# Where the projections of the neighbourhood attention are emitted: behind the first recurrent mixer, or behind the gated recurrence

## The chip, the cores and the metric

The kernel runs on one core of a Trainium2 chip. The metric is the device time of one execution in microseconds (us); the median of three runs of the kernel before is 2086.45 us (2084.6 to 2095.07). TensorE (PE) multiplies matrices, VectorE (DVE), ScalarE (ACT) and GpSimd (POOL) do elementwise work, and DMA queues, issued here mostly by SyncE (SP) and ScalarE, move data between HBM and the on-chip memory.

## The reference

Two blocks run one after the other on 512 tokens of width 1024. The first (a dilated window attention and a gated delta rule) isn't touched here. The second block has three mixers side by side on one normalised input, then an output projection and a mixture of 32 experts. Cut to what matters:

```python
hl = rms_norm(xl, norm1_gain) * (1 + sc1l) + sh1l          # 512 tokens
hc = rms_norm(xc, norm1_gain) * (1 + sc1c) + sh1c          # 256 context tokens
pl, pc = hl @ w_in, hc @ w_in
al, bl, cl = split(pl, [A_PROJ, A_PROJ + B_PROJ])          # hgrn | rwkv | neighbourhood attention
a_lat = hgrn2_mixer(ac, al, ...)        # gated recurrence: chunk_gla in both directions, 4 heads
b_lat = rwkv7_mixer(bc, bl, ...)        # recurrence s = s*w - (s kk) ak + v k, both directions, 4 heads
c_lat = neighbourhood_attention(cc, cl, ...)   # 8 heads: softmax(q k + bias) v over an 8 x 16 window and the context
xl = xl + g1l * (concat([a_lat, b_lat, c_lat]) @ w_out)
xl = xl + g2l * hierarchical_moe(rms_norm(xl, norm2_gain) * (1 + sc2l) + sh2l, ...)
```

## The kernel before

It is one program written with a tile framework: Python emits the operations of each stage, a scheduler with priorities in the order of emission merges them into one fixed order per engine, and rotating buffers of named pools carry the dependencies. Once that order is fixed, every engine runs its own list strictly in order, so work "fills" an idle engine only where it stands in that engine's list between the instructions that wait.

The stages of the second block, in the order of emission:

- `rwkv_in` and `rwkv` (the first recurrent mixer, lines 960 to 1255): the 768 tokens are six blocks. For a block `j`, `front(j)` builds `KR`, `AH` and the matrix `AS` (L1068, L1118, L1120); four stores put `AS` into a scratch buffer (L1125, `rsc<-AS`), one load brings it back spread over all partitions (L1127, `rB<-rsc`); `solve32_rows` inverts it on VectorE in 31 steps of two instructions (L626, L627); four stores and four loads carry the result back into `AS` (L1145 `rsc<-sX`, L1148 `AS<-rsc`). `back(j)` starts with matmuls on that `AS` (L1157) and goes through `merge32` (L648, L652) and the state (L1166 to L1214). `front` runs one block ahead of `back`. A last part normalises and stores rows of `mix` (L1241 to L1255).
- `project` (L1277): the other projections. They are products of 128 output columns with `hl` (512 tokens) and `hc` (256 tokens), each made of three matmuls on split numbers (`mm3`, lines 314 to 316; the weights are split by ScalarE at L299 and GpSimd at L300). In this order: for the neighbourhood attention `w_na` (queries and keys, with sums of squares `nss` by a matmul at L1329) and `w_nv` (values); for the gated recurrence `w_hi` and `w_hg`. All results go to HBM. Being independent of `rwkv`, they are merged among its instructions.
- `hgrn` (the gated recurrence, L1368): loads `hfd`, `hkd`, `hqd`, `hvd`, `hgd`, then two pairs of heads with seven levels each, and a read-out into `mix` (L1545, L1552). Beside its levels runs `out_first`: the part of the output projection whose rows of `mix` are ready (weights `wor`, L1720; `g<-mrh,woh`).
- `na` (the neighbourhood attention): `prepare(p)` for four pairs of heads (tables `ntab`, loads `nt`, `nvt`, `nvw`, `nb`; lines 1562 to 1612), then four units a pair of scores (`ns`, L1637, L1639), softmax (`np`, L1643 on), transpose (`nT`, L1655) and values (`no`, L1670). `prepare(0)` is called from inside `hgrn` at its tenth step (`na_beside`).
- the rest of the output projection (`out_projection`), the router, and the experts, whose 201 MB of weights (`er`) stream in from 1542 us on.

The PSUM pool `gp` holds three buffers for the tag `g`, handed out in the order of emission: a projection can't begin before the buffer three tiles back is read out.

Of the kernel before, what the change touches and what calls it, by code (L numbers as in the profile page):

```python
# [10 lines left out]
F32 = mybir.dt.float32  # L11
F32R = mybir.dt.float32r
I32 = mybir.dt.int32
AF = mybir.ActivationFunctionType
# [125 lines left out]
def consts2():  # L140
    c = Pack()
    i = np.arange(P)
    c.add("ident", np.eye(P))
    bones = (i[:, None] // 64 == i[None, :] // 64).astype(np.float32)
    c.add("bones64", bones / 64)

    s, t = (i % 64)[:, None], np.arange(64)[None, :]
    c.add("rw_mask", np.concatenate([s < t, s <= t], 1).astype(np.float32))
    m = np.ones(T)
    m[63::64] = 0  # L150
    c.add("rw_reset", np.broadcast_to(m, (P, T)))
    sel = np.zeros((P, 4, 32))
    for h in range(8):
        sel[64 * (h % 2):64 * (h % 2) + 64, h // 2, h] = 1 / 64
    c.add("na_sel", sel)
    return c


def consts3():
    c = Pack()  # L160
    i = np.arange(P)
    c.add("ident", np.eye(P))
    c.add("bones64", (i[:, None] // 64 == i[None, :] // 64) / 64)
# [7 lines left out]
    f = np.arange(TC) % P  # L171
    c.add("hg_suf", np.broadcast_to((f != P - 1).astype(np.float32), (P, TC)))
    c.add("hg_pre", np.broadcast_to((f != 0).astype(np.float32), (P, TC)))
    return c
# [65 lines left out]
def prep2(i):  # L240
# [4 lines left out]
    o["c2"], o["c3"] = C2.array(), C3.array()  # L245
# [27 lines left out]
class Kern:  # L273
# [698 lines left out]
    def rwkv_in(self):  # L972
# [4 lines left out]
        nc.vector.tensor_scalar(m2, mu, 0.5, None, OP.mult)  # L977
        self.rw_wl = rw.tile([P, 768], F32, name="wlo")
# [41 lines left out]
    def rwkv(self):  # L1020
# [35 lines left out]
        def front(j):  # L1056
# [19 lines left out]
            nc.vector.tensor_tensor_scan(es[:, ::-1], sg[:, 1:T + 1][:, ::-1], self.c("rw_reset")[:, ::-1], 0.0, OP.add, OP.mult)  # L1076
# [34 lines left out]
            mask = self.c("rw_mask")  # L1111
# [165 lines left out]
    def project(self):  # L1277
# [4 lines left out]
        self.hqd, self.hgd = dram("hqd", 2, P, T), dram("hgd", 2, P, T)  # L1282
        self.hfd, self.hkd, self.hvd = dram("hfd", 2, 2, P, N), dram("hkd", 2, 2, P, N), dram("hvd", N, 256)
        self.nqk, self.nkc, self.nvd = dram("nqk", 4, 2, P, T), dram("nkc", 4, P, TC), dram("nvd", TC, T)
        self.nvw = dram("nvw", 4, 4, 64, 2, P)
        self.nqr, self.nkr = dram("nqr", 8, T), dram("nkr", 8, N)
# [33 lines left out]


# [18 lines left out]
        tokens(I["w_hi"], lambda i, o: rows(self.hvd, i, o))  # L1340


        l = self.v("lb")
        lb, nb = (self.gs.tile([P, 4], F32, name=n) for n in ("hlb", "hnb"))
        nc.vector.tensor_sub(lb, l, l)
        nc.scalar.activation(lb, lb, AF.Exp)
        nc.vector.reciprocal(nb, lb)
        nc.vector.tensor_mul(lb, lb, nb)
        nc.vector.tensor_sub(lb, lb, lb)
        nc.vector.tensor_scalar(nb, lb, -1.0, 1.0, OP.mult, OP.add)  # L1350
        for p in range(2):
            columns(I["w_hg"][p], self.hqd[p])
        for p in range(2):
            for d in range(2):
                c = 2 * d + p
                ps = self.gemm2(I["w_hg"][2 + c])
                f, k = st(N), st(N)
                for o, sign in ((f, 1.0), (k, -1.0)):
                    for x, t in zip((o[:, :TC], o[:, TC:]), ps):
                        nc.scalar.activation(x, t, AF.Sigmoid, scale=sign)  # L1360
                nc.vector.tensor_scalar(f, f, nb[:, c:c + 1], lb[:, c:c + 1], OP.mult, OP.add)
                nc.vector.tensor_scalar(k, k, nb[:, c:c + 1], None, OP.mult)
                nc.sync.dma_start(self.hfd[p, d], f)
                nc.sync.dma_start(self.hkd[p, d], k)
        for p in range(2):
            columns(I["w_hg"][8 + p], self.hgd[p], func=AF.Silu)

    def hgrn(self):  # L1368
# [167 lines left out]
        self.heads = self.na()  # L1536
        for i, p in enumerate(self.h_order):
            next(steps[p], None)
            for _ in range(self.na_beside.count(i)):
                next(self.heads)  # L1540
# [170 lines left out]
    def out_first(self):  # L1711
# [519 lines left out]
    def run(self):  # L2231
# [5 lines left out]
        self.na_beside = [9]  # L2237
# [9 lines left out]
        with ExitStack() as es:  # L2247
# [19 lines left out]
            with ExitStack() as e2:  # L2267
                for n in ("p2", "gs"):
                    pool(e2, n)
                pool(e2, "gp", 3, space=PSUM)  # L2270
                with ExitStack() as e3:
                    pool(e3, "tw")
                    self.block2_in()
                right.close()
                right = es.enter_context(ExitStack())
                pool(right, "rw", side="right")
                for n, b in (("rmp", 2), ("rcp", 2)):
                    pool(right, n, b, space=PSUM, side="right")
                self.rwkv_in()
                self.wq = nc.scalar  # L2280
                self.rwkv()
                self.project()
            ew.close()
            pool(es, "pc3")
            self.cst, self.cat = self.pc3.tile([P, C3.n], F32, name="c3"), C3.at
            nc.gpsimd.dma_start(self.cst, self.I["c3"])
            self.wq = nc.sync
            left = es.enter_context(ExitStack())
            pool(left, "nw")
            right.close()  # L2290
            pool(left, "nmp", space=PSUM)
            with ExitStack() as e2:
                e3 = e2.enter_context(ExitStack())
                pool(e3, "tl", side="right")
                with ExitStack() as e4:
                    pool(e4, "o1", side="right")
                    self.x = self.tl.tile([P, KD, T], F32, name="x1b")
                    self.out_at = (1, 1), (1, 1), (1, 3), (1, 3), (1, 5), (1, 5), (1, 6)
                    with ExitStack() as e5:
                        pool(e5, "hw", side="right")  # L2300
                        pool(e5, "hmp", 4, space=PSUM, side="right")
                        self.hgrn()
                e4 = e3.enter_context(ExitStack())
# [10 lines left out]
                left.close()  # L2314
# [31 lines left out]
```

## Time and profile before

| | |
|---|---|
| median of three runs | 2086.45 us |
| the profiled execution | 2096.92 us, span 2094.9 us |
| PE busy | 1841.7 us (88% of the span) |
| DVE, ACT, POOL busy | 970.0, 676.9, 579.8 us |
| chain that ended last | PE 32%, DMA 16%, issue 11%, DVE 7% |

The profile gives one execution of the program. A page of it has busy time by engine, the span in slices, and the chain of work that ended last, followed back from the last instruction. All times of the rows below are microseconds from the start of the span. "PEclk" is the granted clock of TensorE as a share of 2.4 GHz; "DMA share" is the mean busy share of the 16 DMA engines. Matmuls overlap in their pipeline, so the pace of a row of them is read from their starts, not from their durations. The profiled execution is 10.5 us longer than the median of the runs.

### The profile page before, as it was taken

To read this page: it belongs to the slowest core of one execution; us is meant where nothing else is said; L and a number is where in the kernel's file an instruction comes from. 1 tells how busy PE (TensorE), PEld (TensorE's weight loads), DVE (VectorE), ACT (ScalarE), POOL (GpSimd) and SP (SyncE) were. 2 spreads that over 40 slices of the span, in tenths; PEclk is the share of its full clock that TensorE was granted. 3 is DMA by queue.
4 is the path that set the end of the run, shared out by engine and by line. 5 is a ranking of instruction groups with operands and counts; after the bars stand their busy time and mean duration, and the time that the engine had idled before them with its cause. 6 is when DMAs were issued, how large, how long until landed. Compare 5 with 4: busy or idle time off the path is not lost.

```text
span 2094.9 us, 30479 instructions
## 1 busy us (share of the span) xinstructions
PE 1841.7 (88%) x11941; PEld 1304.6 (62%) x11941; DVE 970.0 (46%) x2047; ACT 676.9 (32%) x1246; POOL 579.8 (28%) x407
## 2 busy tenths in 40 slices
PE   5988899889899999889998999558896999999986
PEld 4665576666657777767687877436675554545442
DVE  5433643676673116435666544577666322222110
ACT  6662325543443234442232214534332111000000
POOL 3222412343446554341111111562101100101011
PEclk9877799899989999998778779669997999999999
DMA  3111223455642335222212123723356899999997
GB/s 131 41 50 36 76 61 112 131 177 192 199 141 78 94 109 191 64 81 70 66 37 68 44 64 96 245 94 116 100 221 260 324 412 415 414 416 412 415 413 278
DMA packets 132862, 363.69 MB, mean 174 GB/s; under 512 B 44110, under 2 KB 63726, under 8 KB 108014
## 3 DMA queue, kind: packets, MB, share of 16 engines
q1 hardware_dynamic: 122206, 340.86, 44.2%
q10 hardware_dynamic: 5472, 15.05, 2.6%
q0 software_dynamic: 5040, 5.82, 1.4%
q8 instruction: 95, 1.56, 0.3%
q14 instruction: 49, 0.40, 0.1%
HBM read 333.02 MB, written 26.55 MB: 172 GB/s over the span
## 4 chain that ended last, share of the span: by engine, by line
PE 32%; DMA 16%; issue 11%; DVE 7%; ACT 4%; POOL 4%; SPq 0%; POOLq 0%; ACTq 0%; DVEq 0%
DMA out_dram<-ey,sidx 13%; PE g L316 6%; PE g L314 6%; PE g L315 6%; DVE sX L627 1%; PE rm L1118 1%; POOL lo L300 1%; DVE stmp L626 1%; PE rm L1068 1%; PE gu L2144 1%; ACT hi L299 1%; DMA wor<-in_w_o_dram 1%; PE tr L2080 1%; DMA nt<-nqk 1%; PE no L1670 1%
## 5 line engine op out<-in xcount | busy, mean ns | idle before, releaser
L300 POOL TENSOR_TENSOR lo<-wraw,hi 128x1024 fp32r<-128x1024 f32 (+1 forms) x127 | 299.1, 2356 | 587.1 <-ACT hi L299 516.7
L314 PE MATMUL g<-h1hi,hi 128*128 128x512 f32 (+1 forms) x584 | 253.7, 434 | 11.7 <-ACT gt L441 7.5
L316 PE MATMUL g<-h1hi,lo 128*128 128x512 f32 (+1 forms) x584 | 250.7, 429 | 6.6 <-POOL lo L300 6.6
L315 PE MATMUL g<-h1lo,hi 128*128 128x512 f32 (+1 forms) x584 | 253.0, 433 | 3.1 <-DVE h1lo L357 1.6
L2144 PE MATMUL gu<-er,xw 128*64 128x256 f32 x2048 | 237.6, 382 | 11.3 <-DMA er<-in_w_e_dram 10.0
L299 ACT ACTIVATE hi<-wraw 128x1024 fp32r<-128x1024 f32 (+1 forms) x127 | 127.4, 1004 | 315.1 <-PE g L315 172.6
L2144 PEld LDWEIGHTS gu<-er,xw 128*64 128x64 f32 x2048 | 145.3, 137 | 98.8 <-issue 17.8
L2173 POOL DMA_INDIRECT out_dram<-ey,sidx x32 | 49.9, 1561 | 454.0 <-DVE ey L2172 454.0
L314 PEld LDWEIGHTS g<-h1hi,hi 128*128 128x128 f32 (+1 forms) x584 | 118.6, 203 | 46.9 <-ACT gt L441 8.4
L316 PEld LDWEIGHTS g<-h1hi,lo 128*128 128x128 f32 (+1 forms) x584 | 117.8, 202 | 44.4 <-POOL lo L300 11.4
L315 PEld LDWEIGHTS g<-h1lo,hi 128*128 128x128 f32 (+1 forms) x584 | 118.1, 202 | 38.4 <-issue 8.7
L2169 PE MATMUL py<-er,es 128*64 128x512 f32 x512 | 121.3, 606 | 1.5 <-SPq L2215 1.0
L314 PE MATMUL g<-hlhi,hi 128*128 128x512 f32 x200 | 85.2, 426 | 4.7 <-ACT hlhi L951 4.6
L2147 ACT ACTIVATE eg<-gu 128x256 f32<-128x256 f32 x32 | 12.2, 384 | 238.8 <-PE gu L2144 238.8
L2080 PE MATMUL tr<-h,S 128*128 128x512 f32 x256 | 75.0, 423 | 12.3 <-DVE xw L2089 7.1
L316 PE MATMUL g<-hlhi,lo 128*128 128x512 f32 x200 | 85.2, 426 | 0.0
L315 PE MATMUL g<-hllo,hi 128*128 128x512 f32 x200 | 85.2, 426 | 0.0
L2172 DVE SCALAR_TENSOR_TENSOR ey<-py,wslot,g2row 128x512 f32<-128x512 f32 x32 | 24.0, 751 | 120.5 <-PE py L2169 120.5
L2169 PEld LDWEIGHTS py<-er,es 128*64 128x64 f32 x512 | 34.3, 137 | 61.4 <-issue 53.3
L2148 DVE TENSOR_TENSOR eh<-eg,gu 128x256 f32<-128x256 f32 x32 | 13.3, 417 | 127.0 <-ACT eg L2147 127.0
L2080 PEld LDWEIGHTS tr<-h,S 128*128 128x128 f32 x256 | 46.1, 196 | 39.6 <-issue 20.5
L898 DVE CUSTOM_DVE_ANT_0 aw<-aw,acc 128x1024 f32<-128x1024 f32 x48 | 64.7, 1354 | 8.1 <-DMA aw<-in_w_ada_dram 7.8
(658 smaller groups left out, 3700.5 us busy)
## 6 DMA issues: line engine op xcount, KB each, us to landing
er<-in_w_e_dram SPq DMA_DIRECT2D x192, 1024.0 KB
aw<-in_w_ada_dram SPq DMA_DIRECT2D x48, 512.0 KB
wraw<-in_w_qkv_dram SPq DMA_DIRECT2D x36, 512.0 KB
wraw<-in_w_g_dram SPq DMA_DIRECT2D x12, 512.0 KB
dxs<-draw SPq DMA_DIRECT2D x96, 64.0 KB
wraw<-in_w_rw_dram SPq DMA_DIRECT2D x9, 512.0 KB
wraw<-in_w_ga_dram SPq DMA_DIRECT2D x8, 512.0 KB
wraw<-in_w_gb_dram SPq DMA_DIRECT2D x8, 512.0 KB
```

The costliest lines, as they stand in the source:

```text
L299: nc.scalar.activation(hi, raw, AF.Copy)
L300: (lo_engine or nc.gpsimd).tensor_sub(lo, raw, hi.bitcast(F32))
L314: nc.tensor.matmul(ps, lh, rh, start=start, stop=False, **kw)
L315: nc.tensor.matmul(ps, lh, rl, start=False, stop=False, **kw)
L316: nc.tensor.matmul(ps, ll, rh, start=False, stop=stop, **kw)
L626: nc.vector.tensor_mul(t, X[:, 0:m, u:u + 1].to_broadcast([P, m, w]), B[:, u:u + 1, u + 1:].to_broadcast([P, m, w]))
L898: nc.vector.tensor_tensor_reduce(out=w, in0=w, in1=cc, scale=1.0, scalar=0.0, op0=OP.mult, op1=OP.add, accum_out=self.modl[:, m:m + 1])
L2080: nc.tensor.matmul(ps[:n], S[:, i, :n], self.h2[i][a][:, c], start=i + a == 0, stop=i + a == 4)
L2144: nc.tensor.matmul(ps[64 * c:64 * c + 64, a, :], xs(2 * i + k), w[:, k, a, c, :], start=i + k + a == 0, stop=i == 3 and k == 1 and a == 1, ...
L2169: nc.tensor.matmul(py[64 * c:64 * c + 64], hs[:, k, 64 * i:64 * i + 64], part[:, k, c, :], start=i + k == 0, stop=i + k == 2)
L2172: nc.vector.scalar_tensor_tensor(y, py, w, self.g2, OP.mult, OP.mult)
L2173: nc.gpsimd.indirect_dma_start(out=self.O["out_0"].rearrange("t (h d) -> (t h) d", h=2), out_offset=bass.IndirectOffsetOnAxis(ap=idx, axis ...
```

## The change

`project` gets an argument. `project(True)` stands where `project()` stood and emits only `w_hi` and `w_hg`. `project(False)` emits `w_na`, the sums and `w_nv` after `hgrn()`. The constants `c3`, the pools of `na` and its first step (`prepare(0)`), which were emitted ahead of `hgrn` or inside it, come after that. `out_first` takes its PSUM tiles from `gp` (three buffers, shared with the projections) in place of two of `nmp`, since `nmp` is opened later. The constants `rw_mask` and `rw_reset` get an array of their own, loaded in `rwkv_in`; two constants of `hgrn` move to the array that is loaded first.

```diff
+def consts_rw():
+    s, t = (np.arange(P) % 64)[:, None], np.arange(64)[None, :]
+    m = np.ones(T)
+    m[63::64] = 0
+    return np.concatenate([s < t, s <= t, np.broadcast_to(m, (P, T))], 1).astype(np.float32)
...
+        self.rw_c = rw.tile([P, P + T], F32, name="rwc")
+        nc.sync.dma_start(self.rw_c, I["c_rw"])
...
-            mask = self.c("rw_mask")
+            mask = self.rw_c[:, :P]
...
-    def project(self):
+    def project(self, first):
...
+        if first:
...
+            tokens(I["w_hi"], lambda i, o: rows(self.hvd, i, o))
...
+            for p in range(2):
+                columns(I["w_hg"][8 + p], self.hgd[p], func=AF.Silu)
+            return
...
         for hf in range(2):
             tokens(I["w_nv"][2 * hf:2 * hf + 2], lambda i, o: window_rows(hf, i, o))
-        tokens(I["w_hi"], lambda i, o: rows(self.hvd, i, o))
...
-        self.heads = self.na()
-        for i, p in enumerate(self.h_order):
+        for p in self.h_order:
             next(steps[p], None)
-            for _ in range(self.na_beside.count(i)):
-                next(self.heads)
...
-            ps = [self.nmp.tile([P, T], F32, tag="ns", name=self.name("g"), bufs=2) for _ in range(2)]
+            ps = [self.gp.tile([P, T], F32, tag="g", name=self.name("g")) for _ in range(2)]
...
-                self.project()
-            ew.close()
-            pool(es, "pc3")
...
+            self.rwkv()
+            self.project(True)
+            right.close()
...
                         self.hgrn()
+                        self.project(False)
+                        ew.close()
+                        self.wq = nc.sync
+                        pool(left, "pc3")
...
+                        pool(nl, "nmp", space=PSUM)
+                        self.heads = self.na()
+                        next(self.heads)
```

What this moves in the engines' lists is not seen in the diff. Three places matter.

The first is TensorE's list where `back` of the fourth block (counted from one) begins in `rwkv`; `g` are projection tiles, `hlhi` and `hllo` the split input, `rm`, `pw`, `px` belong to the recurrence. Before:

```order
L1157 MATMUL rm_8277<-c_5995,AS_7690 32x32 x16
L314 MATMUL g_9866<-hi_9870,hlhi 128x256
L315 MATMUL g_9866<-lo_9871,hlhi 128x256
L316 MATMUL g_9866<-hi_9870,hllo 128x256
...
L648 MATMUL pw_8296<-rXT_8276,AS_7690 32x32 x8
```

The same place now (`_8279` is the same tile under its new number):

```order
L584 MATMUL rm_8152<-c_5995,rt_8150 64x64
L586 MATMUL rm_8152<-c_5995,rt_8150 64x64
L1161 MATMUL rm_8279<-c_5995,AS_7692 32x32 x16
L650 MATMUL pw_8298<-rXT_8278,AS_7692 32x32 x8
L654 MATMUL px_8300<-AS_7692,rt_8299 32x32 x8
```

The projections that remain have run out: from `back` of the third block to the end of `rwkv` no projection matmul is left in the list.

The second is the end of `hgrn` on TensorE, where `hm` are its last matmuls. Before, the scores `ns` of the neighbourhood attention stand between them:

```order
L1524 MATMUL hm_11171<-hPT_10625,hvt 64x128 x2
L1637 MATMUL ns_11352<-nk_10945,nq_10935 128x256
L1637 MATMUL ns_11353<-nk_10945,nq_10935 128x256
L1499 MATMUL hm_11206<-c_10448,hE_10538 128x128 x4
L1499 MATMUL hm_11213<-c_10448,hE_10539 128x128 x3
L1527 MATMUL hm_11172<-hlf_10478,hS_11136 64x128
```

Now:

```order
L1530 MATMUL hm_10343<-hPT_9839,hvt 64x128 x3
L1530 MATMUL hm_10343<-hPT_9840,hvt 64x128 x4
L316 MATMUL g_10488<-hlhi,hi_10484 128x512
L1505 MATMUL hm_10378<-c_5995,hE_9753 128x128 x4
L1533 MATMUL hm_10344<-hlf_9693,hS_10308 64x128
```

`g_10488` is the first tile of the moved projections. This is the first of its 24 matmuls in the list; nine more of them stand among the last of `hgrn`, and the other fourteen and the matmuls of all the other moved tiles stand behind the last matmul of `hgrn`. Between the seven levels there is none, only the 48 of `out_first`.

The third is SyncE's list, which issues the loads beside `hgrn`. Before, the loads of the neighbourhood attention stand among the weights `wor` of `out_first`:

```order
L1720 DMA wor_10780<-in_w_o_dram 128x256
L1720 DMA x1b<-x1d 128x512
L1562 DMA ntab<-in_c_na_dram 128x1024
L1588 DMA nt_10930<-nqk 128x512
L1591 DMA nt_10931<-nqr 128x1x512
...
L1612 DMA nvw_11345<-nvw 128x1x256 x4
L1720 DMA wor_10786<-in_w_o_dram 128x256
```

Now:

```order
L1723 DMA x1b<-x1d 128x512 x4
L1723 DMA wor_9995<-in_w_o_dram 128x256
L1723 DMA x1b<-x1d 128x512
L1723 DMA wor_10001<-in_w_o_dram 128x256
L1723 DMA wor_10115<-in_w_o_dram 128x256
L1723 DMA wor_10121<-in_w_o_dram 128x256
L1555 DMA mix<-ho_10369 128x512
```

The `wor` loads now follow one another, and `ntab` and the first `nt` stand behind the last store of the moved projections.

## Rows read from the trace of the kernel before

**Rows 1.** Windows: busy us (count) of PE, PEld, DVE, ACT, POOL; clock; DMA share.

```profile
915.00:1080.00 165.00, 154.28 (x1050) 112.56 (x1048) 96.89 (x261) 56.76 (x105) 27.66 (x28) 0.80 0.23 62
1080.00:1312.00 232.00, 217.81 (x2036) 182.11 (x2036) 128.86 (x364) 65.67 (x110) 38.38 (x32) 0.85 0.23 65
...
1343.00:1434.00 91.00, 57.92 (x484) 47.52 (x484) 68.20 (x109) 35.20 (x83) 53.72 (x63) 0.74 0.35 112
1434.00:1542.00 108.00, 96.75 (x658) 65.70 (x656) 72.18 (x148) 51.49 (x104) 18.36 (x10) 0.95 0.31 92
...
1600.00:2090.00 490.00, 445.71 (x2996) 242.71 (x2992) 107.77 (x198) 43.35 (x95) 49.94 (x32) 0.99 0.97 391
```

**Rows 2.** Waits of DVE, 1080 to 1320 us: total, times, longest.

```profile
DVE rXT L1160 <- PE rm L1157: 25.5, 3, 18.6
```

**Rows 3.** The chain in order of time, in `rwkv`: start, us, what.

```profile
1091.48 10.03 DMA rB<-rsc
...
1267.05 2.81 DMA rsc<-sX
1270.01 1.66 DMA AS<-rsc
...
1290.45 0.96 PE rm L1213 x26
...
1316.09 7.12 DMA hlf<-hfd
```

**Rows 4.** The chain in `hgrn`.

```profile
1358.64 0.68 POOL ntab L1568
...
1362.27 2.21 POOL ntab L1568 x2
...
1368.55 1.18 POOL ntab L1568
...
1382.19 4.57 DMA wor<-in_w_o_dram
...
1395.95 9.22 DMA wor<-in_w_o_dram
```

**Rows 5.** Line L1157, first matmuls of `back`: third block, then sixth.

```profile
L1157 PE MATMUL rm<-c,AS x32: 191/191/212, 1108.2 to 1110.6; 32*32 32x32 f32 x32
...
L1157 PE MATMUL rm<-c,AS x32: 185/191/212, 1271.8 to 1274.0; 32*32 32x32 f32 x32
```

**Rows 6.** Timeline of PE, projections: start, us, line, tiles.

```profile
924.24 0.39 PE L314 MATMUL g<-hlhi,hi 128*128 128x512 f32 x1
924.47 0.39 PE L315 MATMUL g<-hllo,hi 128*128 128x512 f32 x1
...
925.04 0.28 PE L315 MATMUL g<-hclo,hi 128*128 128x256 f32 x1
925.15 0.28 PE L316 MATMUL g<-hchi,lo 128*128 128x256 f32 x1
...
936.64 1.04 PE L1329 MATMUL nss<-gst,c 128*32 128x512 f32 x2 [1.88 <-ACT gst L1328]
```

**Rows 7.** Groups by line, DVE, 915 to 1295 us.

```profile
L627 DVE TENSOR_TENSOR sX<-sX,stmp 128x60 f32<-128x60 f32 (+24 forms) x186 | 51.9, 280 | 5.0
L626 DVE TENSOR_TENSOR stmp<-sX,rB 128x60 f32<-128x60 f32 (+24 forms) x186 | 44.9, 242 | 6.8 <-DMA rB<-rsc 1.9
```

**Rows 8.** The chain in the neighbourhood attention.

```profile
1451.62 1.88 DVE nst L1645
...
1458.26 12.64 DMA nt<-nqk
1470.92 0.69 DVE nt L1602
```

**Rows 9.** Line L1643, first step of the softmax.

```profile
L1643 DVE CUSTOM_DVE_ANT_1 np<-ns,nb x28: 675/685/692, 1430.7 to 1530.5; 128x512 f32<-128x512 f32 x28
```

**Rows 10.** Windows: granted clock in a back of the recurrence.

```profile
1040.00:1060.00 20.00, 20.00 (x180) 13.78 (x178) 3.40 (x11) 2.86 (x7) 0.40 (x1) 0.50 0.12 30
```

More of the change, by code (lines that the diff above doesn't have):

```diff
@@ L145, in consts2 @@
     c.add("bones64", bones / 64)
[L147 to L151, printed above, removed]
     sel = np.zeros((P, 4, 32))
@@ L155, in consts2 @@
     c.add("na_sel", sel)
-    return c
+    f = np.arange(TC) % P
+    c.add("hg_suf", np.broadcast_to((f != P - 1).astype(np.float32), (P, TC)))
+    c.add("hg_pre", np.broadcast_to((f != 0).astype(np.float32), (P, TC)))
+    return c
+def consts_rw():
[3 more added lines that the diff above has]
+    return np.concatenate([s < t, s <= t, np.broadcast_to(m, (P, T))], 1).astype(np.float32)
 def consts3():
@@ L170, in consts3 @@
     c.add("rt_half", np.broadcast_to((i[:, None] >= 64), (P, 48)).astype(np.float32))
-    f = np.arange(TC) % P
-    c.add("hg_suf", np.broadcast_to((f != P - 1).astype(np.float32), (P, TC)))
-    c.add("hg_pre", np.broadcast_to((f != 0).astype(np.float32), (P, TC)))
     return c
@@ L244, in prep2 @@
     o["xcT"] = np.ascontiguousarray(g("ctx")[0].T.reshape(KD, P, TC).transpose(1, 0, 2))
-    o["c2"], o["c3"] = C2.array(), C3.array()
+    o["c2"], o["c3"], o["c_rw"] = C2.array(), C3.array(), consts_rw()
     o["v2"] = vecs2(i).array()
@@ L1075, in front @@
             es, si = tmp(T), tmp(T)
-            nc.vector.tensor_tensor_scan(es[:, ::-1], sg[:, 1:T + 1][:, ::-1], self.c("rw_reset")[:, ::-1], 0.0, OP.add, OP.mult)
+            nc.vector.tensor_tensor_scan(es[:, ::-1], sg[:, 1:T + 1][:, ::-1], self.rw_c[:, P:][:, ::-1], 0.0, OP.add, OP.mult)
             nc.vector.tensor_add(si, es, sg[:, :T])
@@ L1281, in project @@
         dram = lambda n, *s: self.dp.tile(list(s), F32, name=n)
[L1282 to L1286, printed above, removed]
         def st(n):
@@ L1319, in columns @@
             return o
+        if first:
+            self.hqd, self.hgd = dram("hqd", 2, P, T), dram("hgd", 2, P, T)
+            self.hfd, self.hkd, self.hvd = dram("hfd", 2, 2, P, N), dram("hkd", 2, 2, P, N), dram("hvd", N, 256)
+            tokens(I["w_hi"], lambda i, o: rows(self.hvd, i, o))
+            l = self.v("lb")
+            lb, nb = (self.gs.tile([P, 4], F32, name=n) for n in ("hlb", "hnb"))
+            nc.vector.tensor_sub(lb, l, l)
+            nc.scalar.activation(lb, lb, AF.Exp)
+            nc.vector.reciprocal(nb, lb)
+            nc.vector.tensor_mul(lb, lb, nb)
+            nc.vector.tensor_sub(lb, lb, lb)
+            nc.vector.tensor_scalar(nb, lb, -1.0, 1.0, OP.mult, OP.add)
+            for p in range(2):
+                columns(I["w_hg"][p], self.hqd[p])
+            for p in range(2):
+                for d in range(2):
+                    c = 2 * d + p
+                    ps = self.gemm2(I["w_hg"][2 + c])
+                    f, k = st(N), st(N)
+                    for o, sign in ((f, 1.0), (k, -1.0)):
+                        for x, t in zip((o[:, :TC], o[:, TC:]), ps):
+                            nc.scalar.activation(x, t, AF.Sigmoid, scale=sign)
+                    nc.vector.tensor_scalar(f, f, nb[:, c:c + 1], lb[:, c:c + 1], OP.mult, OP.add)
+                    nc.vector.tensor_scalar(k, k, nb[:, c:c + 1], None, OP.mult)
+                    nc.sync.dma_start(self.hfd[p, d], f)
+                    nc.sync.dma_start(self.hkd[p, d], k)
+            for p in range(2):
+                columns(I["w_hg"][8 + p], self.hgd[p], func=AF.Silu)
+            return
+        self.nqk, self.nkc, self.nvd = dram("nqk", 4, 2, P, T), dram("nkc", 4, P, TC), dram("nvd", TC, T)
+        self.nvw = dram("nvw", 4, 4, 64, 2, P)
+        self.nqr, self.nkr = dram("nqr", 8, T), dram("nkr", 8, N)
         sums = self.gp.tile([96, T], F32, tag="ss", name="nss", bufs=1)
@@ L1339, in project @@
             tokens(I["w_nv"][2 * hf:2 * hf + 2], lambda i, o: window_rows(hf, i, o))
-        tokens(I["w_hi"], lambda i, o: rows(self.hvd, i, o))
[L1343 to L1366, printed above, removed]
     def hgrn(self):
@@ L2236, in run @@
         self.h_order = [0, 1] * 9
-        self.na_beside = [9]
         self.mixed = None
@@ L2266, in run @@
                 self.block1_tail()
[L2267 to L2281, printed above, removed]
-                self.project()
-            ew.close()
-            pool(es, "pc3")
-            self.cst, self.cat = self.pc3.tile([P, C3.n], F32, name="c3"), C3.at
-            nc.gpsimd.dma_start(self.cst, self.I["c3"])
-            self.wq = nc.sync
+            e2 = ew.enter_context(ExitStack())
+            for n in ("p2", "gs"):
+                pool(e2, n)
+            pool(e2, "gp", 3, space=PSUM)
+            with ExitStack() as e3:
+                pool(e3, "tw")
+                self.block2_in()
+            right.close()
+            right = es.enter_context(ExitStack())
+            pool(right, "rw", side="right")
+            for n, b in (("rmp", 2), ("rcp", 2)):
+                pool(right, n, b, space=PSUM, side="right")
+            self.rwkv_in()
+            self.wq = nc.scalar
+            self.rwkv()
+            self.project(True)
+            right.close()
             left = es.enter_context(ExitStack())
-            pool(left, "nw")
-            right.close()
-            pool(left, "nmp", space=PSUM)
             with ExitStack() as e2:
@@ L2302, in run @@
                         self.hgrn()
+                        self.project(False)
+                        ew.close()
+                        self.wq = nc.sync
+                        pool(left, "pc3")
+                        self.cst, self.cat = self.pc3.tile([P, C3.n], F32, name="c3"), C3.at
+                        nc.gpsimd.dma_start(self.cst, self.I["c3"])
+                        nl = left.enter_context(ExitStack())
+                        pool(nl, "nw")
+                        pool(nl, "nmp", space=PSUM)
+                        self.heads = self.na()
+                        next(self.heads)
                 e4 = e3.enter_context(ExitStack())
@@ L2313, in run @@
                     self.out_projection(k, k + 1)
-                left.close()
+                nl.close()
                 self.er_bufs = 14
```

## The prediction

> **What bounds the kernel now.** I read the windows by stage first [rows 1]. From 1600 us on the DMA engines are busy 0.97 of the time: the experts' weights set the pace, so whatever is won or lost before the first of them is issued moves the end by as much, and no more. Before that, TensorE looks like the limit: it is busy 217.81 of 232 us in the second half of the first recurrent mixer and 96.75 of 108 in the neighbourhood attention, but only 57.92 of 91 beside the gated recurrence, whose levels leave it idle. A busy engine isn't yet one that sets the end, though. In the first mixer much of that work is projections laid between instructions that wait for others. So I read next who waits for whom there: VectorE waited 25.5 us in three places for the first matmuls of `back` to be done [rows 2], which stand in TensorE's list among projections. Last I read the chain, for the steps that neither engine can shorten: scratch stores and loads around the triangular solve [rows 3], and in the gated recurrence the waits for `wor` and the table `ntab` [rows 4].
>
> The change takes the projections of the neighbourhood attention out of the first mixer. The order says that they don't fill the gated recurrence either: only ten matmuls of the first tile stand among its last ones. The reason is the pool: `gp` has three buffers given out as emitted, the eight tiles of `out_first` come first, and the last of these is emitted at the second pair's last level but one. So the sum is: what the mixer and the gated recurrence gain, against about 100 us of TensorE work that has nothing beside it.
>
> **Part by part.**
>
> A. The first mixer. Up to `back` of the third block, at 1108.2 us [rows 5], both lists still hold projections. After it the new list is bare. In the old one, matmuls worth 87 us at full pace are left there: the whole list has 385 projection matmuls of 512 columns and 624 of 256; with starts 0.227 us apart (0.23 as printed) for 512 columns and 0.12 for 256 [rows 6] these take 87 and 73 us, and the sums `nss` some 10 more, 170 in all, of which 83 stand ahead of this place. What they really hold up is the spacing of the blocks. The third to the sixth `back` start within 1271.8 − 1108.2 = 163.6 us [rows 5], 54.5 a block. Bare, a block's loop is: solve, 186 instructions of each of two lines over six blocks, (51.9 + 44.9)/6 = 16 us [rows 7]; store, load and start of `back`, 2.81 + 1.66 and the queue's issue between, 7 us; four stores of `AS` for the next block, about as long as the four of `sX`, 3 us; the load `rB` 10.03 us [rows 3], rounded up to 12 since in SyncE's list it now stands behind the previous block's `AS` load; and some 4 us of other VectorE instructions that stand among the solve's. That is 42 us. A floor is VectorE's own work: 96.89 + 128.86 us in the two windows, a sixth of it 37 us [rows 1, 7]. A ceiling is 48, if the state's matmuls fall into line with the solve instead of lying beside it. Three spacings: 126 instead of 163.6, −38 (−53 to −16). The third block itself starts some 4 earlier. Behind the last `back` matmuls at 1290.45, the read-out and the loads of `hlf` at 1316.09 [rows 3] have 37 projection matmuls between their steps in the old list, 37 × 0.23 = 8 us. Together −50, with −28 and −68 as ends.
>
> B. The handover. `hlf` took 7.12 us to come [rows 3]; the stores it reads are done long before in the new order, and fewer stores share the queue. −4 (0 to −7).
>
> C. Beside the gated recurrence. In the old list of SyncE the loads of the neighbourhood attention stand between those of `wor`; the chain waited 4.57 and 9.22 us for `wor` and had 0.68 + 2.21 + 1.18 = 4.1 us of `ntab` on GpSimd [rows 4], which is the engine that carries the levels. All of this goes, 18 us. Late next is the chain on GpSimd and VectorE of each level, which stays. I take −15 (−22 to −8), as a part of `wor`'s wait was beside level work that is needed anyway.
>
> D. The projections behind the gated recurrence. 192 matmuls of 512 columns at 0.227 us are 43.6; 96 for the context's keys and 288 for the values, of 256 columns at 0.12, are 46.1. The twelve sums come in six pairs of 1.04 us, and before a pair stands a wait of 1.88 for ScalarE's square [rows 6]; with four such waits, 13.7. Sum +103. Ten matmuls lie in the end of `hgrn`, 2 us, which I leave in for the start-up. At the least 98 (two waits), at the most 118 (all waits, and a late buffer in `gp`). Nothing in the old kernel paid for this on the path: it was the filling. What lies beside it now is only the read-out of `hgrn`.
>
> E. `prepare(0)`. In the old kernel it was done beside the gated recurrence. Now tables, loads and rotations stand between the last projection and the first score. A load of `nt` with its queue took 12.64 us [rows 8]; the table's GpSimd work 4.1 [rows 4]; nine VectorE instructions like the 0.69 one 6.2 [rows 8]; the last two steps on `nk` some 3 us. That is 26. In the list 26 matmuls of the output projection stand there, 26 × 0.23 = 6 us, which were elsewhere before. So +20 (12 if half of the load hides behind them and the projections' end, 26 if they wait too).
>
> F. The neighbourhood attention itself. Old, its softmax ran from 1430.7 to 1530.5 [rows 9], and the stage was over at 1542. In the beginning the read-out of `hgrn` stood between its instructions: the second unit's reduction came only at 1451.62 [rows 8], some 20 us after the first score. That read-out and the 26 matmuls are now done before. −19 (0 to −35, the latter if the wait of 12.64 goes as well). And since the projections can start only at the end of `hgrn`, 1434, while the scores started at 1430.7, +3.
>
> The rest: a new load of 128 × 640 numbers (0.33 MB) in `rwkv_in`, where the queues have room (DMA share 0.23 [rows 1], 1 us if it should not be hidden); constants that change place, nothing; three buffers in place of two for `out_first`, nothing, since `wor` and not PSUM held it.
>
> Sum: −50 − 4 − 15 + 103 + 20 − 19 + 3 = +38. The profiled execution took 2096.92 us, 10.5 above the median of the runs; the forecast is put on the median, 2086.45 + 38 = 2124 (a profiled execution would be near 2135).
>
> **The clock.** In a stretch of the recurrence the granted clock was 0.50 while TensorE was busy all 20 us [rows 10], and 0.85 over the window of A [rows 1]. Own matmuls of the recurrence are 217.81 less the 87/0.85 = 102 us of projections, 116 us. If they all ran at 1.2 GHz they would take 116 × 0.85/0.5 = 197, 81 more; a bit under half of them, `back`, is on the loop, +33. The Trainium skill (TensorE: Matmul & The Clock Gate, What's actually happening) says that the array's clock has these two levels only and the throttled one is the default, released by how busy the array has been lately. By that rule the bare mixer runs at 1.2 GHz throughout; by the row alone it did so even with projections present, in which case A needs no correction. R2 below prices it.
>
> **Rivals.**
>
> R1, the other side: the first mixer was bound by TensorE, so all of the 102 us comes out of it, not 50. For it: 217.81 of 232 busy. Then the whole is −102 − 4 − 15 + 103 + 20 − 19 + 3 = −14, 2072. It decides when the spacing of the last blocks falls below 30 us. Against it: VectorE's 37 us a block and the 42 of the scratch loop.
>
> R2: the bare mixer falls to 1.2 GHz and A is −50 + 33 = −17: +71, 2157. For it [rows 10]; against it, that the clock is already low there.
>
> R3: the neighbourhood attention gains nothing, F = 0, and E is 26, because the loads of `nvw`, `nb` and `nt` for the second pair now start with those of the first instead of beside the gated recurrence: +63, 2149. For it: the wait of 12.64 [rows 8].
>
> R4: the change balances. With A at −68, C at −22, F at −35, and E at 12, −68 − 4 − 22 + 98 + 12 − 35 + 3 = −16; half way between that and the forecast lies +11, so 2086 to 2097 needs most terms at their near ends; taken as 2090.
>
> R5, that the change doesn't do what it says, is no rival but my forecast: the moved matmuls are not fillers.
>
> **How the numbers follow.** Forecast 0.48, R2 0.17, R3 0.14, R4 0.12, R1 0.09. A measurement can tell about 0.5%, 10 us. Slower holds the forecast, R2, R3: 0.79. Same: R4, 0.12. Faster: R1, 0.09. The likeliest case by itself spans 2095 to 2150, the terms' ends taken together as independent. The range for 8 in 10 goes from 2083 to 2165, which leaves out R1 and the far ends.
>
> **What would show it.** Right: 40 to 45 us between the last `back`s, TensorE's busy share in that stretch falling to about half; the gated recurrence with no `wor` wait over 2 us; then a block of some 100 us of bare projections at a clock near 1, and some 20 us with TensorE nearly idle before the first score; the first `er` load near 1580. Wrong: spacings above 50 (A), projections found between the levels, or a first `er` load before 1545, by which the change would be no loss.

## The result and the profile after

The changed kernel takes 2233.24 us (median of four runs, 2225.57 to 2235.3) against 2090.76 for the kernel before beside it: ratio 1.0668 (95% interval 1.0635 to 1.07), 142 us slower. The forecast was 38 us slower, 2124, with a range up to 2165: the direction was right, the size was not. The profiled execution took 2225.57 us, 128.65 more than the one of before, and 128.8 of these had passed when the first expert weights were issued (1542.1 before, 1670.9 after); the experts behind it are the same. The stages below therefore account for 129 of the 142 us: the profiled execution is the fastest of the changed kernel's four, and the one of before lies 6 us above its median.

Cut at instructions that both kernels have, from the first or last start of their lines:

| stage (us) | before | after | change | forecast |
|---|---|---|---|---|
| start to the third `back` | 1108.2 | 1111.7 | +3.5 | −4 |
| third to sixth `back` | 163.6 | 138.7 | −24.9 | −38 |
| sixth `back` to the last store of `mix` | 39.6 | 39.5 | −0.1 | −8 |
| to the first level of `hgrn` | 31.6 | 31.2 | −0.4 | −4 |
| to the last matmul on `hS` | 96.0 | 76.5 | −19.5 | −15 |
| to the first score's softmax | −8.3 | 142.4 | +150.7 | +126 |
| first to last softmax | 99.8 | 119.2 | +19.4 | −19 |
| to the first `er` load | 11.6 | 11.7 | +0.1 | 0 |

The windows of the changed kernel, columns as in [rows 1]:

```profile
1080.00:1292.00 212.00, 127.97 (x1394) 101.75 (x1390) 108.54 (x356) 41.42 (x72) 13.88 (x19) 0.62 0.12 31
...
1317.00:1398.00 81.00, 58.21 (x522) 48.52 (x523) 55.53 (x95) 41.64 (x95) 47.55 (x59) 0.83 0.10 31
1398.00:1500.00 102.00, 95.07 (x544) 77.08 (x544) 6.92 (x11) 38.72 (x51) 32.16 (x17) 0.98 0.34 108
1500.00:1540.00 40.00, 21.28 (x101) 17.41 (x102) 9.03 (x15) 1.79 (x3) 5.18 (x6) 0.65 0.48 139
1540.00:1660.00 120.00, 74.14 (x524) 52.34 (x523) 56.62 (x133) 36.23 (x83) 12.15 (x8) 0.78 0.29 91
```

In the mixer TensorE is busy 60% of the time, and its clock has fallen from 0.85 to 0.62. From 1398 to 1500 it does the bare projections at 0.98; their last matmul starts at 1506.5. In the 40 us to the first score TensorE is busy 21 us, at 0.65, and VectorE, the next, 9. Then follows an attention phase with TensorE at 62%, where it was 90% [rows 1].

The third and the sixth `back` start at (compare [rows 5]):

```profile
L1161 PE MATMUL rm<-c,AS x32: 191/191/213, 1111.7 to 1112.2; 32*32 32x32 f32 x32
...
L1161 PE MATMUL rm<-c,AS x32: 228/236/254, 1250.4 to 1252.0; 32*32 32x32 f32 x32
```

The chain through one block of the bare mixer (compare [rows 3]):

```profile
1165.15 1.02 PE rm L1161 x32
...
1181.64 0.75 PE rc L1193 x14
...
1186.14 0.64 PE rm L1072 x4
...
1205.94 0.69 DVE AS L1124
...
1208.91 1.96 DMA rsc<-sX
1212.89 8.47 DMA rB<-rsc
```

Here the reader sees three parts one behind the other: `back` from 1165 to 1186, the next `front` from 1186 to 1206, then the stores of the solved block (`rsc<-sX`) and its load back into `AS`, and at 1213 the next `back`. The load `rB` that is issued then belongs to the block after. The solve isn't a part by itself: in VectorE's list its steps stand among those of `back` and `front`, and it runs from 1174.5 to 1206.9:

```profile
1174.51 0.18 DVE L628 TENSOR_TENSOR stmp<-sX,rB 128x31 f32<-128x31 f32 x1
...
1206.74 0.17 DVE L629 TENSOR_TENSOR sX<-sX,stmp 128x8 f32<-128x8 f32 x1
```

VectorE's wait for `back`'s first matmuls is no shorter than in [rows 2], although no projection stands ahead of the last three of the four:

```profile
DVE rXT L1164 <- PE rm L1161: 35.4, 4, 11.9
```

Beside the gated recurrence `wor` is waited for less; the same view gave 23.4 us in three waits before:

```profile
ACT woh L301 <- DMA wor<-in_w_o_dram: 6.5, 2, 5.2
```

The chain ahead of the first score and through the attention phase (compare [rows 8]):

```profile
1512.56 11.93 DMA nt<-nqr
...
1532.77 11.17 DMA nvw<-nvw
1544.32 16.19 DMA nt<-nkr
...
1568.18 18.53 DMA nt<-nkr
...
1604.72 17.36 DMA nt<-nkr
```

Three loads of the norms of the keys, one a pair, hold 52 of the phase's 119 us. In the kernel before, three of the four such loads were issued ahead of the first score at 1430.7 [rows 9], the last of them here:

```profile
1427.08 0.50 SPq L1591 DMA_DIRECT2D nt<-nkr  x1
```

In the changed kernel only the first pair's is. The softmax steps (compare [rows 9]):

```profile
L1646 DVE CUSTOM_DVE_ANT_1 np<-ns,nb x28: 676/685/692, 1540.0 to 1659.2; 128x512 f32<-128x512 f32 x28
```

### The profile page after: what moved, and what is told of

Its sections match the earlier page's. It is cut to its first block, busy times and chain, and to the rows that moved or that the text cites. A ratio compares the mean times of both kernels' runs of the same rounds, so it can differ in the third digit from the quotient of the medians.

```text
span 2223.5 us, 30525 instructions
## 1 busy us (share of the span) xinstructions
PE 1849.1 (83%) x11941; PEld 1316.7 (59%) x11941; DVE 941.6 (42%) x2047; ACT 688.6 (31%) x1255; POOL 575.0 (26%) x407
## 4 chain that ended last, share of the span: by engine, by line
DMA 18%; PE 18%; issue 10%; DVE 6%; ACT 3%; POOL 2%; SPq 1%; POOLq 0%; ACTq 0%; DVEq 0%
DMA out_dram<-ey,sidx 12%; DMA nt<-nkr 2%; PE g L317 2%; PE g L316 2%; PE g L318 2%; PE rm L1122 1%; DMA rB<-rsc 1%; DVE sX L629 1%; DVE stmp L628 1%; PE gu L2147 1%; PE rm L1072 1%; PE tr L2083 1%; PE rc L1201 1%; PE no L1673 1%; PE rm L584 1%
## 5 line engine op out<-in xcount | busy, mean ns | idle before, releaser
L2083 PEld LDWEIGHTS tr<-h,S 128*128 128x128 f32 x256 | 46.0, 196 | 39.7 <-issue 20.5
```

The costliest lines, as they stand in the source:

```text
L2083: nc.tensor.matmul(ps[:n], S[:, i, :n], self.h2[i][a][:, c], start=i + a == 0, stop=i + a == 4)
```

## The experiments

Stage times (us) of each, cut as in the table above, from one profiled execution. "To the store" is the read-out, from the sixth `back` to the last store of `mix`; "gap" runs from the last matmul on `hS` to the first score's softmax.

| | 3rd to 6th `back` | to the store | `hgrn` | gap | attention |
|---|---|---|---|---|---|
| before | 163.6 | 39.6 | 96.0 | −8.3 | 99.8 |
| changed | 138.7 | 39.5 | 76.5 | 142.4 | 119.2 |
| all_behind | 163.0 | 38.9 | 76.0 | 34.4 | 123.7 |
| na_behind | 161.7 | 43.3 | 76.2 | 70.4 | 120.1 |
| eighth | 140.3 | 40.9 | 76.5 | 97.6 | 117.2 |
| fill | 139.0 | 39.7 | 162.6 | 35.2 | 124.8 |
| nt8 | 140.2 | 41.6 | 74.9 | 143.5 | 113.8 |
| norm_set | 138.5 | 39.8 | 76.4 | 143.3 | 81.1 |
| after_nt | 139.8 | 40.8 | 76.0 | 139.9 | 80.9 |
| after_split | 136.1 | 39.8 | 76.4 | 138.6 | 74.3 |

**Where the projections stand.** all_behind moves one call back:

```diff
             self.project(True)
+            self.project(False)
...
                         self.hgrn()
-                        self.project(False)
```

> All projections stand behind the first mixer again, those of the gated recurrence first; only the first step of the neighbourhood attention stays behind the gated recurrence. Theory 1 (the lost time is in two places, the bare projections and a preparation whose loads start late): the mixer takes its old time, the gated recurrence stays some 17 us shorter, the gap before the first score is some 35 us and the attention itself some 19 us longer than before: about 2125 us. Rival (the late preparation costs nothing by itself, the projections alone do): near 2075, attention phase 100 us as before.

2159.44 us, ratio 1.0318 (1.0288 to 1.0348). More than expected: no projection is bare, and still 67 us are lost. The gated recurrence keeps its 20 us, but the preparation behind it costs 34.4 + 8.3 = 42.7 us before the first score, and the attention phase is no shorter than in the changed kernel. The rest of the gap, 142.4 − 34.4 = 108 us, is what the bare projections cost.

na_behind leaves only the values (`w_nv`) behind the gated recurrence:

```diff
             self.project(True)
+            self.project(False)   # w_na and the sums
...
-                        self.project(False)
+                        self.project(None)   # w_nv
```

> Queries and keys behind the first mixer again (some 60 us of matmuls), values behind the gated recurrence. Theory 1 with the bare mixer bound by its own serial loop (back, front, store and load of AS) at the lower clock: the spacing of the last blocks is nearly as with no projections, 46 to 50 us, and 60 us less stand bare: about 2175 us. Rival (each projection matmul in the mixer costs its own time there): spacing above 52, total above 2200.

2192.51 us, 1.0476 (1.0433 to 1.0519). The values cost 70.4 − 34.4 = 36.0 us bare, and their 288 matmuls at 0.12 us are 34.6: the price of a bare matmul is its pace. But the spacing was 161.7: the 60 us of queries and keys cost these spacings 23 us, so this part of the expectation failed. At the end of this mixer the projections have run out, while in all_behind they have not. The same code, from the sixth `back` to the last store, na_behind first and then all_behind:

```profile
1290.20:1333.50 43.30, 26.37 (x272) 17.22 (x272) 15.52 (x30) 16.34 (x20) 2.76 (x4) 0.66 0.04 14
```

```profile
1284.90:1323.80 38.90, 36.55 (x422) 30.17 (x422) 15.52 (x30) 19.29 (x24) 7.37 (x6) 1.00 0.12 36
```

With 150 matmuls fewer it takes 4.4 us longer, at a clock of 0.66 instead of 1.00. The clock alone isn't shown to be the cause: the other bare read-outs of the table take 39.5 to 41.6 us at 0.63 to 0.72, and the kernel before takes 39.6 with projections at 1.00. What these show is that the projections between the matmuls of the read-out cost nothing there.

eighth sums one slice of eight in the moved projections and leaves out the others:

```diff
-            for k in range(KD):
+            for k in range(self.deep):   # 1 in project(False), else KD
```

> The changed kernel, but the moved projections sum over one of their eight slices of the contraction, so seven eighths of their matmuls are left out; loads, splits and stores stay. Theory 1 (their matmuls stand bare and set the pace): some 75 of 90 us go, about 2155 us, and the attention phase behind stays 119 us. Rival (stores, weight splits and loads set the pace between the gated recurrence and the first score): under 40 us go, over 2190.

2179.53 us, 1.0414 (1.0341 to 1.0487). The gap fell by 44.8 us, between the two expectations: with the matmuls nearly gone it is still 97.6 − 34.4 = 63 us longer than without projections. Its chain shows what is next, weight loads, splits and stores of results one after another:

```profile
1433.77 4.97 DMA nqk<-gst
...
1440.47 2.37 POOL lo L302
1442.86 3.57 DMA wraw<-in_w_nv_dram
```

fill hands out the moved projections a piece after each step of `hgrn`:

```diff
+        moved = self.project_steps(False)
         for p in self.h_order:
             next(steps[p], None)
+            next(moved, None)
```

> The moved projections are emitted a piece at a time between the steps of the gated recurrence, so that they stand among its levels. Theory 1: TensorE was free for some 25 to 30 us there; that much is hidden, the levels get a few us longer, the rest stays bare: about 2205 us. Rival A: the buffers of gp are held by out_first and nothing moves, 2230. Rival B: it all fits in, 2150.

2217.03 us, 1.0593 (1.0562 to 1.0624). Now they do stand among the levels, but 162.6 + 35.2 against 76.5 + 142.4 is only 21 us less. The levels pay: VectorE waits for their scores, which stand behind projections.

```profile
DVE hPT L1473 <- PE hm L1464: 58.2, 7, 15.0
```

**The bare mixer.** warm adds matmuls that nobody reads, three at each of four places of a block:

```diff
+    def warm(self, j, a, n=3):
+        if j < 3:
+            return
+        ps = self.gp.tile([P, T], F32, tag="g", name=self.name("g"))
+        for k in range(n):
+            self.nc.tensor.matmul(ps, a[:, :P], a, start=k == 0, stop=k == n - 1)
```

> The changed kernel with extra matmuls of 128x512 whose result nobody reads, twelve a block from the fourth block of the first mixer on, each on a tile that the recurrence has just made. Theory 1 (the bare mixer is slow because its own matmuls run at 1.2 GHz): the granted clock there rises from 0.57 to over 0.75 and the last three spacings stay at 139 us or fall, although some 10 us of work a block were added. Rival (the clock is of no account, the loop through scratch memory and VectorE sets the spacing): the clock may rise, the spacings stay. Rival (TensorE's own work sets it): each block gets some 10 us longer.

2264.9 us, 1.0804 (1.0736 to 1.0872): the extra tiles of `gp` also pushed the projections of the gated recurrence behind the mixer, so only the stretch from the third to the sixth `back` is of use, in which no projection ran at all:

```profile
1076.60:1208.00 131.40, 97.75 (x1079) 69.06 (x1079) 77.58 (x260) 18.86 (x45) 4.62 (x11) 0.73 0.08 17
```

The same stretch of the kernel before, and of the changed kernel:

```profile
1108.20:1271.80 163.60, 152.24 (x1458) 129.37 (x1459) 88.24 (x262) 36.49 (x70) 25.53 (x20) 0.80 0.22 60
```

```profile
1111.70:1250.40 138.70, 81.11 (x1026) 68.94 (x1026) 77.94 (x282) 23.25 (x49) 8.48 (x12) 0.59 0.10 25
```

With more work on TensorE the stretch is 7 us shorter than in the changed kernel, at 0.73 instead of 0.59. But the two don't hold the same work: VectorE has 260 instructions in one and 282 in the other, since in warm a load `rB` and the first steps of the solve on it lie ahead of the third `back`, and in the changed kernel behind it. Warm first, then the changed kernel:

```profile
1061.87 9.26 DMA rB<-rsc
```

```profile
1114.99 10.36 DMA rB<-rsc
```

From the fourth to the sixth `back` both have 182, warm first:

```profile
1123.40:1208.00 84.60, 67.31 (x711) 44.49 (x711) 50.88 (x182) 11.38 (x26) 1.94 (x3) 0.77 0.09 21
```

```profile
1165.10:1250.40 85.30, 49.63 (x658) 42.58 (x658) 48.88 (x182) 11.45 (x26) 3.25 (x3) 0.58 0.09 20
```

So the spacings stay, with 18 us more on TensorE. The rival by which each block gets 10 us longer is out. Between the other two the run doesn't decide: the added work may have cost what the clock gave back, or the clock may be of no account. One line of `back` tells more. Its 32 matmuls, in the fourth, fifth and sixth block of the kernel before:

```profile
1173.72 1.90 PE rm L1166 x32
...
1240.38 1.90 PE rm L1166 x32
...
1279.41 1.08 PE rm L1166 x32
```

In the changed kernel they take 1.93 us in each of these blocks, and in warm 1.90 in the fourth and the fifth; the fifth of either:

```profile
1224.27 1.93 PE rm L1170 x32
```

```profile
1179.99 1.90 PE rm L1180 x32
```

While they ran, the clock was at 1.00 (2.4 GHz) in the sixth block of the kernel before, where TensorE had been busy for 39 of the 41 us of the block ahead, and in all the others at 0.50, the lower of its two levels (1.2 GHz). So on this line the fourth and fifth `back` ran at the lower level with projections among them, too, the unread matmuls didn't raise it there, and only the sixth lost by the change.

**The attention phase.** nt8:

```diff
-tag="nt", name=self.name("nt"), bufs=4)
+tag="nt", name=self.name("nt"), bufs=8)
-tag="nx", name=self.name("nx"), bufs=1)
+tag="nx", name=self.name("nx"), bufs=2)
```

> The changed kernel with eight buffers instead of four for the loads nt and two instead of one for nx; the pool is opened after the gated recurrence's is closed, to have the room. Theory 1a (a pair's loads can't be issued before the pair ahead has given its buffers back): the attention phase falls from 119 to about 100 us, total 2212. Theory 1b (the transfers themselves are slow, and earlier ones only queue up): the phase stays over 112 us or the first score comes later by as much, total 2225 to 2235.

2227.64 us, 1.0626 (1.0558 to 1.0695), phase 113.8: 5 us of it, so it is not the buffers in the main.

norm_set fills in ones for the norms of three pairs:

```diff
-                nc.sync.dma_start(rb, norm[2 * p:2 * p + 2, None, :].to_broadcast([2, 64, n]))
+                if p:
+                    nc.gpsimd.memset(rb, 1.0)
+                else:
+                    nc.sync.dma_start(rb, norm[2 * p:2 * p + 2, None, :].to_broadcast([2, 64, n]))
```

> The changed kernel, where for the second to fourth pair the broadcast loads of the norms (nt from nqr and nkr) are replaced by a fill with ones on GpSimd: that part of the normalisation is left out, the buffers and their order stay. Theory 1b (these transfers set the pace): the attention phase falls from 119 to some 90 us, total about 2200. Theory 1a (buffers): over 110 us, total over 2222.

2193.86 us, 1.0465 (1.0397 to 1.0533), phase 81.1: the loads are the 38 us. after_norm_pe makes the norms by matmuls with ones and zeros (and, to make room, has three buffers `nt` instead of four and one constant of `hgrn` in place of two), and says the same with nothing left out:

```diff
+                for r, w, to in (((64, TC, 0), (32, T, TC)) if a else ((0, T, 0),)):
+                    pb = psum("ns", 2)
+                    nc.tensor.matmul(pb[:, :w], one[r:r + 8], self.nrs[r:r + 8, :w], start=True, stop=True)
+                    nc.scalar.activation(rb[:, to:to + w], pb[:, :w], AF.Copy)
```

> The changed kernel with the norms by matmul for all four pairs. Theory 1b (the broadcast loads are the cause of the longer attention phase): the phase falls from 119 to some 85 us as it did with the fill of ones, and the gap before the first score falls by some 10 us, since the first pair's broadcasts go too: total about 2187. Rival (the fill helped because the work on the norms was left out): the phase stays over 110 us.

2207.18 us, 1.0578 (1.0528 to 1.0627): phase 81.3, but the gap rose to 151.0 instead of falling. So without the first pair's broadcasts the gap is no shorter; its chain has the loads of the bias `nb` and the halves `nx`:

```profile
1526.64 9.01 DMA nb<-in_b_na_dram
1536.80 11.07 DMA nb<-in_b_na_dram
1548.25 6.34 DMA nx<-nqk
```

Why is such a load slow? While the changed kernel waits for one, from 1569 to 1580, the DMA line and the rate (40 slices of the window) are:

```profile
DMA  8611112795711111111111111111111111111111
GB/s 242 216 63 52 37 52 74 216 276 186 268 30 37 45 60 45 45 60 45 45 60 45 45 60 45 45 60 41 56 48 45 48 45 56 45 56 45 56 45 56
```

About 50 GB/s, where all sixteen engines move 391 in [rows 1]: an eighth, two engines. The load's outermost dimension is 2. The load of the queries' norms, issued at 1563.9, has the same outermost dimension and lies ahead of it: at 50 GB/s the 256 + 384 KB of both take some 13 us, an estimate, of the 22.8 until the second has landed at 1586.7. after_nt issues it as two loads, the same bytes from the same rows:

```diff
+                for i in range(2):
+                    nc.sync.dma_start(rb[64 * i:64 * i + 64], norm[2 * p + i:2 * p + i + 1, :].to_broadcast([64, n]))
```

> The changed kernel, each broadcast load of the norms issued as two loads of 64 partitions from one row instead of one load whose outer dimension is 2; the same bytes from the same rows. Theory 2 (a load uses as many DMA engines as its outermost dimension counts): the loads take some 4 us instead of 16, the attention phase falls from 119 to about 84 us, total 2194. Rival (one row of HBM read by 64 partitions is slow, or the queue is full): the phase stays over 110 us.

2199.79 us, 1.0515 (1.0458 to 1.0571), with the phase at 80.9:

```profile
L1647 DVE CUSTOM_DVE_ANT_1 np<-ns,nb x28: 673/684/693, 1542.3 to 1623.2; 128x512 f32<-128x512 f32 x28
```

This settles it: neither the row of HBM nor the queue, but the shape. (In after_split below, which has the same two loads, those into `nt` land 3.0 to 6.9 us after they are issued, 4.3 in the median.) The Trainium skill says so (DMA: Bandwidth & Descriptors, Rules for kernel authors): an outermost dimension below 16, such as a leading broadcast, confines a load to at most that many engines. The trace agrees, with 50 GB/s for 2.

after_split does the same to `rB` and `nvw` (outermost dimension 4):

```diff
+            for h in range(4):
+                nc.sync.dma_start(B[32 * h:32 * h + 32].rearrange("p r c -> p (r c)"), dsc.rearrange("q g r c -> (q g) (r c)"))
...
+                for r in range(4):
+                    nc.sync.dma_start(vw[32 * r:32 * r + 32, j], self.nvw[p, r, k0:k0 + 32])
```

> As after_nt, and the loads rB (outer dimension 4) and nvw (4) are split in four each. Theory 2: rB takes some 5 instead of 10 us in each block of the bare mixer, so the three last spacings fall from 139 to about 125 us, and the gap before the first score falls by some 10 us: total about 2165. Rival (rB is hidden behind VectorE's other work, and more issues on SyncE cost as much): 2190 or more.

2180.37 us, 1.0422 (1.0374 to 1.047): phase 74.3, but the spacings 136.1 instead of 125, and the gap 138.6. The total lies between the two expectations. `rB` now lands 2.3 to 3.5 us after it is issued, and the bare mixer gains 3 us: its loop doesn't hang on these loads.

**Is there something for the kernel before?** norm_pe, before_rb and before_split put the edits of after_norm_pe, of `rB` alone and of after_split into the kernel before; norm_pe_wa is norm_pe with wor_act, which is

```diff
-            load(raw, I["w_o2"][m][:, 2 * P:4 * P], after)
+            load(raw, I["w_o2"][m][:, 2 * P:4 * P], after, nc.scalar)
```

> The kernel before, but the loads of wor are issued by ScalarE instead of SyncE, so that they don't stand behind the loads of the neighbourhood attention. If that queue cost the gated recurrence its 20 us: some 10 us faster than before, 2080. Rival (ScalarE's own list holds the loads up, or the waits were hidden anyway): no change within 0.5%.

0.9972 (0.9934 to 1.0011).

> The kernel before, but the norms reach all partitions by a matmul with ones and zeros (three a pair) and a copy by ScalarE, instead of by a broadcast load from HBM; three buffers nt instead of four to make room. If the broadcast loads set the pace of the attention phase in this kernel too: the phase falls from 100 to some 82 us, total 2072. Rival (in this kernel the loads of two pairs lie beside the gated recurrence and the others are hidden): within 0.5% of before.

0.9976 (0.995 to 1.0002), the phase at 95.4.

> As norm_pe, and the loads of wor by ScalarE as in wor_act. If both gains add up: some 6 us less than norm_pe, 2066. Rival (with the broadcast loads gone, wor no longer waits in SyncE's list): the same as norm_pe.

1.0006 (0.9981 to 1.0031).

> The kernel before, with only the load rB split in four. If the loop through scratch memory ends last there too: 5 us in some of six blocks, 2075. Rival (TensorE's list with projections sets the spacing): within 0.5%.

1.0054 (1.003 to 1.0079).

> The kernel before with rB, the norms and nvw split. Theory 2: what rB gives, some 10 us in the attention phase and some 5 beside the gated recurrence, where nvw blocked SyncE's list: 2065. Rival: these loads are hidden in the kernel before: within 0.5%.

1.0002 (0.9974 to 1.0031). None is faster than can be told from no change, and before_rb is slower by half a per cent. In the profile of before_split the gated recurrence takes 81.1 us instead of 96.0, but the read-out of the mixer 44.2 instead of 39.6 and the attention phase 108.1 instead of 99.8: what one stage gains, the others lose. Why wasn't looked for. No version tried beats the kernel before.

## Why the prediction was wrong

The direction and the main mechanism were right: the moved projections fill nothing and stand bare. D forecast 103 us; all_behind makes it 108. C forecast −15 and was −19.5. Three terms were wrong, and all on the same side.

**F, the attention itself, −19 forecast, +19.4 measured.** The step that failed is that the wait of 12.64 us for `nt` was taken for a remainder that at worst stays. That one was a load of `nqk`, and VectorE stood still for only 2.5 us of it. It has neighbours that the step doesn't count: every pair needs loads of its norms, the kernel before issues three pairs' of them ahead of its first score, and the change leaves the keys' norms of three pairs to the phase, 16 to 19 us each. R3 had the cause, earlier loads that are lost, but priced it at F = 0. With the loads on more engines the phase is 80.9 us, and 99.8 − 19 is 80.8, but this is luck: the −19 keeps the wait of 12.64, and without it the step's own end was −35, 65 us. That the load runs on two engines could have been read from its line in the code and the DMA line of the trace.

**A, the mixer, −50 forecast, −21.5 measured** (+3.5 − 24.9 − 0.1). The step "bare, a block's loop is 42 us" failed. The three spacings are 53.4, 47.8 and 37.5 us, 46.2 in the mean, near the 48 named as a ceiling, and the last has no `front` left in it. In the second, `back` and the next `front` follow one another, 21 and 20 us, then come 6 us of stores and load. The solve's steps stand among theirs and take 32 us, where the sum had them as 16 by themselves; the 12 us of `rB` are not on this path. The step's reading of [rows 2] failed with it: VectorE's waits for `back` are as long without projections ahead, so these weren't the main thing it waited for. The 8 us of the read-out didn't come, 39.5 after 39.6, and the third `back` came 3.5 us later instead of 4 earlier; but there the profiles scatter, 1112 to 1121 us in the bare runs and 1099 to 1118 in the versions of the kernel before. The sizes come near R2, whose A was −17, but its mechanism is not shown: the clock is lower over the three spacings (0.59, before 0.80), yet the line of `back` shown above ran at the lower level in the fourth and fifth block before the change, too. In the sixth block it lost. What the clock costs of the 28 us stays open.

**E, the preparation, 20 forecast (and 3 for the start), 42.7 measured in all_behind.** The step that failed: the table, loads, bias and rotations were added up as one load's wait and some instructions; several loads queue one behind another on one list. Without the broadcasts of the first pair it is no shorter (after_norm_pe). Which load ends last wasn't separated further.

B, −4, was −0.4. The range ended at 2165 since it let the terms err independently. But A, E and F each lie outside their own ends, too: with every term at its worst end the sum is −28 + 0 − 8 + 118 + 26 + 0 + 3 = +111, or 2197. They have one thing in common: each was a sum of single times where the stage hangs on a series of transfers and waits. Two slips of the sums are small: a ceiling of 48 us makes −20 and not −16 of three spacings, and 624 × 0.12 is 75 and not 73.

## What to carry over

Work that fills another stage's idle time is moved at the price of what it covered as well as its own: here the loads prepared beside the gated recurrence cost more (42.7 + 19.4 us) than the mixer gained by losing its fillers (21.5) and the gated recurrence by losing the loads (19.5). Before costing a wait as "hidden now, and hidden later", count how many of its kind there are and where each lies. And a load's time follows its access pattern: compare its rate with that of a full stream, and look at its outermost dimension.

## What was not expected of the hardware

A broadcast load of 384 KB ran at about 50 GB/s beside an idle rest of the DMA engines, and stood 16 to 19 us on the chain, in part behind another of its shape; as two loads of 64 partitions each it left the chain. The read-out of the mixer, a stretch of small matmuls, took 39.5 us by itself at a granted clock of 0.72, and 39.6 us with some 100 matmuls of projections laid between them at 1.00.
